# Stores of an attention-score kernel, given in turn to the SyncE and the ScalarE DMA queue

## Chip, cores and metric

One NeuronCore of a Trainium2 chip runs the kernel. The metric is the device time of one execution in microseconds (us), as the median of several runs; executions of one kernel here mostly agree within 0.3%. A ratio in this text is the mean time of one kernel's fast runs over the mean time of the fast runs of the kernel before, taken in the same rounds on the same chip, so it is not quite the ratio of the medians quoted beside it. "Stretch" means a window of the profiled span, and a "packet" is one piece of a transfer as the profile lists it (16 KB of a store, 8 KB of a load).

## The reference

```python
batch, heads, seq, dim = 8, 8, 512, 64
def reference(q, k):                      # q, k: float32 [8, 8, 512, 64]
    scale = 1.0 / np.sqrt(q.shape[-1])
    return np.einsum('bhqd,bhkd->bhqk', q, k) * scale   # float32 [8, 8, 512, 512]
```

16.8 MB come in, 67.1 MB go out.

## The kernel before

Two batches at a time are a group (4 groups, `v`). Of each group, q and k are loaded (4 loads of 1 MB), cast to bf16 and transposed through TensorE. Then 8 output tiles (`c`) of 2 MB each are computed: TensorE into PSUM (the memory that holds its results), evicted (copied out, and scaled) half by ScalarE and half by VectorE into a tile `o`, and stored with one transfer. There are 5 buffers of `o`. In the text the 32 output tiles are numbered from 0 in program order.

```python
    raw_pool = ctx.enter_context(tc.tile_pool(name="raw", bufs=4))
    out_pool = ctx.enter_context(tc.tile_pool(name="out", bufs=5))
    psum_pool = ctx.enter_context(tc.tile_pool(name="psum", bufs=3, space=bass.MemoryType.PSUM))
    # ... (cut)
    def evacuate(dst, src):               # in turn ScalarE, VectorE
        nonlocal n_evac
        if n_evac % 2 == 0:
            nc.scalar.mul(out=dst, in_=src, mul=scale)
        else:
            nc.vector.tensor_scalar(out=dst, in0=src, scalar1=scale, scalar2=None,
                                    op0=mybir.AluOpType.mult)
        n_evac += 1
    # ... (cut: load_and_cast issues all 16 loads with nc.sync; transpose)
    def scores(v, c, kT, qz):
        o = out_pool.tile([P, RO, S], f32, name="o")
        for i in range(0, RO, 2):
            ps = psum_pool.tile([P, 2, S], f32, name="ps")
            for w in range(2):
                nc.tensor.matmul(out=ps[:, w, :], lhsT=qz[:, i + w, c, :],
                                 rhs=kT[:, c].rearrange("d m j -> d (m j)"),
                                 start=True, stop=True)
            evacuate(o[:, i:i + 2, :], ps)
        nc.sync.dma_start(out=out_r[v, c], in_=o.rearrange("p i k -> p (i k)"))
    # ... (cut: loads of all groups first; transposes of group v + 1 after tile 3 of group v)
```

Of the kernel before, what the change touches and what calls it, by code (L numbers as in the profile page):

```python
# [1 line left out]

# [5 lines left out]


@with_exitstack  # L10
def kernel(
    ctx: ExitStack,
    tc: tile.TileContext,
    q: bass.AP,
    k: bass.AP,
    out: bass.AP,
):






    nc = tc.nc
    B, H, S, D = q.shape
    scale = 1.0 / (D ** 0.5)
    P = 128
    UNITS = B // 2
    N = H // 2
    C = 2 * N  # L30
    M = P // H
    R = S // M
    RO = 8
    U = S // RO
    JJ = R // RO
    IW = 8 // JJ

    f32 = mybir.dt.float32
    bf16 = mybir.dt.bfloat16

    q_r = q.rearrange("(v x) g (m j) d -> v x (g m) (j d)", x=2, j=R)
    k_r = k.rearrange("(v x) g (m j) d -> v x (g m) (j d)", x=2, j=R)
    out_r = out.rearrange("(v x) (n h) (u i) k -> v (x n) (h u) (i k)", x=2, h=2, i=RO)

    consts = ctx.enter_context(tc.tile_pool(name="consts", bufs=1))
    raw_pool = ctx.enter_context(tc.tile_pool(name="raw", bufs=4))
    bf_pool = ctx.enter_context(tc.tile_pool(name="bf", bufs=5))
    t_pool = ctx.enter_context(tc.tile_pool(name="t", bufs=2))
    out_pool = ctx.enter_context(tc.tile_pool(name="out", bufs=5))
    tpsum_pool = ctx.enter_context(tc.tile_pool(name="tpsum", bufs=2, space=bass.MemoryType.PSUM))  # L50
    psum_pool = ctx.enter_context(tc.tile_pool(name="psum", bufs=3, space=bass.MemoryType.PSUM))

    n_evac = 0

    def evacuate(dst, src):
# [8 lines that stand above are left out]
    def load_and_cast(v):  # L64

        both = []
        for src in (k_r, q_r):
            xb = bf_pool.tile([P, R, 2, D], bf16, name="xb")
            for x in range(2):
                xf = raw_pool.tile([P, R * D], f32, name="xf")  # L70
                nc.sync.dma_start(out=xf, in_=src[v, x])  # L71
                if v > 0:
                    copy = nc.gpsimd.tensor_copy
                else:
                    copy = (nc.vector.tensor_copy, nc.scalar.copy)[x]
                copy(out=xb[:, :, x, :], in_=xf.rearrange("p (j d) -> p j d", j=R))  # L76
            both.append(xb)
        return both

    def half(h):  # L80
        return slice(h * D, (h + 1) * D)

    def clear(engine, qz, h):

        engine.memset(qz[half(h), :, :, (1 - h) * U:(2 - h) * U], 0.0)  # L85

    def transpose(v, kb, qb):

        kT = t_pool.tile([P, C, M, R], bf16, name="kT")
        qz = qzs[v % 2]  # L90
        for j0 in range(0, R, 8):
            tp = tpsum_pool.tile([P, 8, P], bf16, name="tp")
            for j in range(8):
                nc.tensor.transpose(out=tp[:, j, :], identity=identity,  # L94
                                    in_=kb[:, j0 + j].rearrange("p x d -> p (x d)"))
            for x in range(2):
                for h in range(2):
                    copy = (nc.vector.tensor_copy, nc.scalar.copy)[h]
                    copy(out=kT[half(h), x * N:(x + 1) * N, :, j0:j0 + 8],  # L99
                         in_=tp[half(x)].rearrange("d j (n h m) -> d h n m j", n=N, h=2)[:, h])  # L100
        for i0 in range(0, RO, IW):
            tp = tpsum_pool.tile([P, IW, JJ, P], bf16, name="tp")
            for i in range(IW):
                for jj in range(JJ):
                    nc.tensor.transpose(out=tp[:, i, jj, :], identity=identity,  # L105
                                        in_=qb[:, RO * jj + i0 + i].rearrange("p x d -> p (x d)"))
            for x in range(2):
                for h in range(2):
                    copy = (nc.vector.tensor_copy, nc.scalar.copy)[h]
                    copy(out=qz[half(h), i0:i0 + IW, x * N:(x + 1) * N, h * U:(h + 1) * U]  # L110
                         .rearrange("d i n (m jj) -> d i n m jj", jj=JJ),
                         in_=tp[half(x)].rearrange("d i jj (n h m) -> d h i n m jj", n=N, h=2)[:, h])
        return kT, qz
# [8 lines that stand above are left out]
                                 rhs=kT[:, c].rearrange("d m j -> d (m j)"),  # L122
                                 start=True, stop=True)
            evacuate(o[:, i:i + 2, :], ps)
        nc.sync.dma_start(out=out_r[v, c], in_=o.rearrange("p i k -> p (i k)"))

    cast = [load_and_cast(0)]
    identity = consts.tile([P, P], dtype=bf16)
    make_identity(nc, identity)
    qzs = [consts.tile([P, RO, C, P], bf16, name=f"qz{n}") for n in range(2)]  # L130
    clear(nc.vector, qzs[0], 0)
    clear(nc.gpsimd, qzs[0], 1)
    for x in range(2):
        clear(nc.gpsimd, qzs[1], x)
    for v in range(1, UNITS):
        cast.append(load_and_cast(v))

    ts = {0: transpose(0, *cast[0])}
    for v in range(UNITS):
        for c in range(C):  # L140
            scores(v, c, *ts[v])
            if c == C // 2 - 1 and v + 1 < UNITS:
                ts[v + 1] = transpose(v + 1, *cast[v + 1])


# [1 line left out]
_INS = ['q', 'k']  # L147
_OUTS = [((8, 8, 512, 512), 'float32')]


# [23 lines left out]
```

## Time and profile before

| | before |
|---|---|
| time, median of 3 | 204.38 us (204.25 to 204.42) |
| profiled span | 203.2 us |
| DMA queue q1, share of 16 engines | 97.3% |
| VectorE, ScalarE, PE busy | 63%, 52%, 52% |
| store, issue to landing | 20.5 us (median) |

No compute engine is busy for more than two thirds of the span, and the one DMA queue for nearly all of it.

### The profile page before, as it was taken

What the parts mean: (1) busy time and instruction counts of PE and PEld (TensorE: products, weight loads), DVE (VectorE), ACT (ScalarE), POOL (GpSimd) and SP (SyncE); (2) the same over time, 40 slices, a digit from 0 to 9 for tenths busy, and PEclk for the clock granted to TensorE, in tenths of its full rate; (3) what the DMA queues carried; (4) which work ended last, traced back from release to release, by engine and by line L of the source; (5) the groups of instructions that cost most, each with busy time, mean ns of one, the idle gap of its engine ahead of it and who ended that gap; (6) DMA issues with size and microseconds to landing.
All of it is one profiled execution on the core that took longest, in us unless ns stands there. A gap on an engine that the chain in (4) does not pass through costs nothing.

```text
span 203.2 us, 1530 instructions
## 1 busy us (share of the span) xinstructions
PE 105.0 (52%) x512; PEld 48.5 (24%) x512; DVE 128.3 (63%) x131; ACT 104.8 (52%) x131; POOL 34.8 (17%) x21
## 2 busy tenths in 40 slices
PE   0033579873388535979555938545455755610000
PEld 0033334332352213533122413112121211200000
DVE  3793778997769989779678889444444444440000
ACT  2317668866676867688384787333333333330000
POOL 8957777706000000000000000000000000000000
PEclk9999999999559999699988699997975597575555
DMA  6999999999999999999999999999999999999990
GB/s 226 427 411 429 421 426 423 419 424 426 432 435 426 435 423 423 439 429 426 435 432 423 435 426 432 435 423 439 429 424 435 426 429 435 429 429 439 423 419 35
DMA packets 6919, 83.98 MB, mean 413 GB/s; under 512 B 768, under 2 KB 768, under 8 KB 768
## 3 DMA queue, kind: packets, MB, share of 16 engines
q1 hardware_dynamic: 6912, 83.89, 97.3%
q8 instruction: 4, 0.07, 0.1%
q14 instruction: 3, 0.02, 0.0%
HBM read 16.78 MB, written 67.11 MB: 413 GB/s over the span
## 4 chain that ended last, share of the span: by engine, by line
DMA 42%; DVE 17%; PE 15%; ACT 13%; issue 1%; SPq 0%; ACTq 0%
DMA out_dram<-o 38%; PE ps L121 9%; DVE o L60 8%; ACT o L58 6%; DMA xf<-in_q_dram 4%; DVE kT L99 4%; ACT kT L99 4%; PE tp L105 4%; DVE qz L110 3%; PE tp L94 3%; ACT qz L110 2%; DVE xb L76 2%; ACT xb L76 1%; SPq L71 0%; ACTq L58 0%
## 5 line engine op out<-in xcount | busy, mean ns | idle before, releaser
L121 PE MATMUL ps<-kT,qz 128*128 128x512 bf16 x256 | 82.3, 450 | 38.2 <-ACT o L58 30.6
L60 DVE TENSOR_SCALAR o<-ps 128x1024 f32<-128x1024 f32 x64 | 77.5, 1223 | 36.2 <-DMA out_dram<-o 22.1
L58 ACT ACTIVATE o<-ps 128x1024 f32<-128x1024 f32 x64 | 63.2, 1022 | 40.7 <-DMA out_dram<-o 34.7
L121 PEld LDWEIGHTS <-qz 128*128 128x128 bf16 x256 | 27.3, 109 | 86.7 <-issue 70.4
L99 ACT COPY kT<-tp 64x512 bf16<-64x512 bf16 x32 | 18.4, 579 | 15.6 <-DVE kT L99 11.6
L110 DVE COPY qz<-tp 64x512 bf16<-64x512 bf16 x32 | 21.5, 686 | 6.5 <-PE tp L105 6.2
L76 POOL CAST xb<-xf 128x2048 bf16<-128x2048 f32 x12 | 22.7, 1893 | 15.5 <-PE tp L94 7.0
L94 PE MATMUL tp<-identity,xb 128*128 128x128 bf16 x128 | 12.5, 261 | 24.0 <-ACT kT L99 11.1
L110 ACT COPY qz<-tp 64x512 bf16<-64x512 bf16 x32 | 18.2, 579 | 12.1 <-DVE qz L110 11.4
L99 DVE COPY kT<-tp 64x512 bf16<-64x512 bf16 x32 | 21.3, 684 | 5.0 <-PE tp L94 4.4
L105 PE MATMUL tp<-identity,xb 128*128 128x128 bf16 x128 | 12.4, 263 | 12.6 <-ACT kT L99 7.3
L94 PEld LDWEIGHTS <-xb 128*128 128x128 bf16 x128 | 10.9, 121 | 27.5 <-issue 16.3
L105 PEld LDWEIGHTS <-xb 128*128 128x128 bf16 x128 | 11.0, 121 | 16.6 <-issue 15.4
L85 POOL MEMSET qz<- 64x4096 bf16 x3 | 11.5, 3830 | 0.1
L76 DVE CAST xb<-xf 128x2048 bf16<-128x2048 f32 x2 | 7.2, 3604 | 3.7 <-DMA xf<-in_k_dram 2.6
L76 ACT CAST xb<-xf 128x2048 bf16<-128x2048 f32 x2 | 3.8, 1897 | 6.1 <-DMA xf<-in_k_dram 6.0
L85 DVE MEMSET qz<- 64x2048 uint32 x1 | 1.8, 1765 | 1.2 <-PEq L158 1.2
L76 ACT ACT_TABLE_LOAD x1 | 1.3, 1283 | 0.7 <-PEq L158 0.7
masks.py:199 POOL TENSOR_SCALAR_AFFINE_SELECT identity<-identity 128x128 bf16<-128x128 bf16 x1 | 0.3, 292 | 0.1
masks.py:197 POOL MEMSET identity<- 128x128 bf16 x1 | 0.2, 204 | 0.3 <-POOLq L158 0.3
L158 POOL MEMSET const-float32-0.0<- 128x1 f32 x1 | 0.1, 103 | 0.2 <-issue 0.2
L158 POOL MEMSET const-bfloat16-1.0<- 128x1 bf16 x1 | 0.1, 111 | 0.0
(2 smaller groups left out, 0.2 us busy)
## 6 DMA issues: line engine op xcount, KB each, us to landing
out_dram<-o SPq DMA_DIRECT2D x32, 2048.0 KB, 20.5
xf<-in_k_dram SPq DMA_DIRECT2D x8, 1024.0 KB, 7.9
xf<-in_q_dram SPq DMA_DIRECT2D x8, 1024.0 KB, 8.4
```

The lines of the kernel that those rows point to most:

```text
L58: nc.scalar.mul(out=dst, in_=src, mul=scale)
L60: nc.vector.tensor_scalar(out=dst, in0=src, scalar1=scale, scalar2=None, op0=mybir.AluOpType.mult)
L76: copy(out=xb[:, :, x, :], in_=xf.rearrange("p (j d) -> p j d", j=R))
L85: engine.memset(qz[half(h), :, :, (1 - h) * U:(2 - h) * U], 0.0)
L94: nc.tensor.transpose(out=tp[:, j, :], identity=identity, in_=kb[:, j0 + j].rearrange("p x d -> p (x d)"))
L99: copy(out=kT[half(h), x * N:(x + 1) * N, :, j0:j0 + 8], in_=tp[half(x)].rearrange("d j (n h m) -> d h n m j", n=N, h=2)[:, h])
L105: nc.tensor.transpose(out=tp[:, i, jj, :], identity=identity, in_=qb[:, RO * jj + i0 + i].rearrange("p x d -> p (x d)"))
L110: copy(out=qz[half(h), i0:i0 + IW, x * N:(x + 1) * N, h * U:(h + 1) * U] .rearrange("d i n (m jj) -> d i n m jj", jj=JJ), in_=tp[half(x)]. ...
L121: nc.tensor.matmul(out=ps[:, w, :], lhsT=qz[:, i + w, c, :], rhs=kT[:, c].rearrange("d m j -> d (m j)"), start=True, stop=True)
L158: nc = _bacc.Bacc("TRN2", target_bir_lowering=False, num_devices=1)
```

## The change

The intent is to spread the stores over two issuing engines, so that neither the issuing nor one queue's order holds them back.

```diff
-        nc.sync.dma_start(out=out_r[v, c], in_=o.rearrange("p i k -> p (i k)"))
+        queue = (nc.sync, nc.scalar)[c % 2]
+        queue.dma_start(out=out_r[v, c], in_=o.rearrange("p i k -> p (i k)"))
```

## The prediction

> **What bounds the kernel now.** I read the page from the fullest resource down: the 40 slices, the DMA queues and issues, the chain that ended last, SyncE's own waits, then a table of stretches for the end. First the slices, queues and issues:
>
> ```profile
> DMA  6999999999999999999999999999999999999990
> GB/s 226 427 411 429 421 426 423 419 424 426 432 435 426 435 423 423 439 429 426 435 432 423 435 426 432 435 423 439 429 424 435 426 429 435 429 429 439 423 419 35
> ...
> q1 hardware_dynamic: 6912, 83.89, 97.3%
> q8 instruction: 4, 0.07, 0.1%
> ...
> out_dram<-o SPq DMA_DIRECT2D x32, 2048.0 KB, 20.5
> ```
>
> The DMA engines stand at nine tenths or more in all slices but the first and the last, and no slice moves more than 439 GB/s. All 16 loads and 32 stores are on one queue, q1, whose packets fill 97.3% of 16 engines' span. A store takes 20.5 us from issue to landing, though 2 MB at 430 GB/s is 4.9 us: some four stores stand in line.
>
> Next, the waits of SyncE (us in total, times, longest):
>
> ```profile
> SPq L125 <- DVE o L60: 132.9, 31, 15.0
> SPq L169 <- DMA out_dram<-o: 20.7, 5, 4.8
> ```
>
> And some steps of the chain that ended last, in order of time (start, length):
>
> ```profile
> 85.33 0.02 SPq L125
> ...
> 85.38 12.88 DMA out_dram<-o
> 98.28 0.04 ACTq L58
> 98.32 0.04 issue
> 98.36 1.03 ACT o L58
> ```
>
> SyncE never waits to issue a store for anything but VectorE's last eviction of that tile: 132.9 us of idle waiting. What it spends on issuing is 32 times some 0.33 us. The chain from 85 us on is a store, an eviction that wanted its buffer, the next store: compute waits for the DMA engines, not they for compute. (Before 85 us the chain runs through compute, but the slices show the DMA engines full there too.)
>
> Last, the stretches at the end (stretch, PE, PEld, DVE, ACT and POOL busy, granted clock, DMA share, GB/s):
>
> ```profile
> 181.00:200.00 19.00, 0.00 (x0) 0.00 (x0) 0.05 (x1) 0.00 (x0) 0.00 (x0) 0.50 0.91 392
> 200.00:201.00 1.00, 0.00 (x0) 0.00 (x0) 0.00 (x0) 0.00 (x0) 0.00 (x0) 0.50 0.08 33
> 201.00:202.00 1.00, 0.00 (x0) 0.00 (x0) 0.00 (x0) 0.00 (x0) 0.00 (x0) 0.50 0.04 16
> ```
>
> Compute ends at 181 us; the last 21 us are the queue emptying. From 200 to 202 us about one engine of 16 (0.06) still works: one engine is behind the others. The trace has 4 packets of 16 KB of instruction fetch, at 38, 70, 106 and 155 us, of 0.88 to 1.11 us each; they sum to 3.8 us, which about fits the 3 us by which one engine outlasts the rest, if all four fell on it.
>
> **What the Trainium skill says.** "DMA: Bandwidth & Descriptors", section "Issuing engines are not separate DMA queues": transfers started from SyncE, ScalarE or GpSimd run on the same 16 engines and interleave; issuing from several saves only the sequencer's time to start them. This trace agrees with the second half as far as one queue can: 0.33 us of issue against 4.9 us of data. Same page, "Queues, rings and completion order": an engine takes turns between the queues that have work, a packet at a time. No run here shows it yet; I use it for the order of landings. Same page, "Where 436 GB/s comes from": 435 GB/s is the ceiling of the 16 ports. The trace agrees: 423 to 439 GB/s, or a median 611 ns for a 16 KB packet, times 16 engines 429 GB/s. "Perfetto Trace Analysis", section "DMA Optimizations", advises spreading over issuing engines when "the bottleneck is descriptor generation"; SyncE's waits above say that it isn't.
>
> **The change, part by part.** Bytes do not change. Per DMA engine a store is 8 packets of 611 ns and a load 8 packets of 309 ns (medians of the trace), so 32 x 8 x 0.611 = 156.4 us and 16 x 8 x 0.309 = 39.6 us, with 48 semaphore packets of 9 ns 0.4: 196.4 us. The first packet starts at 1.75 us, so an undelayed engine ends at 198.2 us; the last one ends at 201.9, its store has landed at 202.4, the span ends at 203.2, and the measured time is 1.2 us more. Of these terms the change touches none: 196.4 of data, 1.75 at the start, 3.7 of the late engine, 2.5 from its last packet to the measured end: 204.4.
>
> What it removes: 16 issues from SyncE, 16 x 0.33 = 5.3 us, all in SyncE's 133 us of idle. Worth 0. It adds them to ScalarE, which is busy 104.8 of 203 us: 5.3 us, 3% of its span. In the stretch from 85 us on ScalarE waits for DMA anyway. Worth 0.
>
> What it moves: ScalarE now executes in order a store that waits for VectorE. In the built order the store of an odd tile stands behind the first eviction of the next tile, some 1 us later, so VectorE's last eviction (1.22 us) is mostly done; but that first eviction itself waits for a buffer. With 5 buffers, three other tiles are then still in the queues, 3 x 4.9 = 14.7 us, so the delay is not seen by the DMA engines. The built schedule also mixes the transposes of the next head group with evictions, where before they stood in a block.
>
> The tightest place is the first turn of the buffers. At 36.6 us, when tile 1's store goes out on ScalarE, about 7.5 us of loads (landing at 44.1) are ahead of tile 0's store on SyncE's queue. Taking turns, tile 1 and then tile 3 pass it. Loads and five stores are 7.5 + 5 x 4.9 = 32 us of work, which ends at 68.4 us in the kernel before (the fifth store's landing), and must here. Tile 0 can land as late as 68.4 - 2 x 4.9 = 58.6, with tiles 2 and 4 behind it (in the built program tile 2's store also waits for tile 1's to have landed); before, it landed at 49.0. Tile 5 wants tile 0's buffer, and its first eviction stands in ScalarE's order before most of the second group's transposes. From 58.6 its path to the store is, on ScalarE, four evictions of 1.02 us (tiles 5 and 6 alternate) and five copies of 0.58: 7.0 us, with some 0.5 us for waits on VectorE and PE, so it issues at about 66.1. An issue's first packet came 1.0 us after it at the start of the kernel (issue 0.75, packet 1.75), so data at 67.1: 1.3 us before the queues are empty. A narrow escape by this estimate; if I have missed 2 or 3 us of waits, a gap of 1 to 2 us opens once. Afterwards a group of 8 tiles needs about 31 us of VectorE (16 x 1.22 + 16 x 0.69) against 39 us of DMA, so the lead grows again. I put 0.3 us into the sum for this, and -0.2 for bubbles between stores that two queues may hide (a store landed every 4.94 us on average against 8 x 0.611 = 4.89, mostly the late engine's). Sum: 204.4 + 0.3 - 0.2 = 204.5 us.
>
> **Rivals.** First, two queues overlap better and it gets faster. [...]Against: [...]the packets cover 97.3% of the span, and the rate is at the port's ceiling. Even with all bubbles and half of the late engine gone it would be some 202 us. Second, blocking in ScalarE's order starves the engines, in the first turn as above or at each group: a gap of 1 to 3 us, one to three times, 206 to 210 us. For: transposes and evictions share ScalarE, and the lead had fallen to 8 us at 60 and 85 us (12.9 us to landing less the store's own 4.9). Against: the lead never fell below that, and work in the queues is conserved whichever is served first. Third, alternating queues makes each packet dearer, or loads and stores mixed disturb each other. 3% on stores would be 156.4 x 0.03 = 4.7 us, so 209. Nothing in this trace speaks for it: the 9 ns semaphore packets already stand between 16 KB ones without a visible gap.
>
> **Range and chances.** The kernel repeats within 0.1%, so the width is mine: low end 203.2 for hidden bubbles, high end 206.8 for one gap of 2 us. Faster by over 2% means under 200.3, which is below 196.4 + 1.75 + 2.5 = 200.7 even with the late engine cured: 1%. Slower by over 2% is above 208.5 and needs a repeated gap or dearer packets: 7%. The rest, 92%, is within 2%.
>
> **What would show it.** Right: two queues with 16-engine shares that sum to 97%, all slices at 9, GB/s as before, store landing still near 20 us, compute ending near 181 us, one late engine at the end. Tile 0's store landing after tile 1's, near 58 us, would confirm the turn-taking. Wrong: a slice under 9 between 60 and 75 us or at a later transposition (second rival); 16 KB packets over 620 ns where both queues are full (third); ScalarE's wait for DMA growing matters only if a slice dips with it.

## More of the kernel before

A scheduler orders each engine's instructions when the kernel is built, and a pool decides then which buffer a tile gets. So a change of one line can move instructions elsewhere.

## The result

| | before | changed |
|---|---|---|
| time, median of 4 | 204.40 us (204.25 to 204.78) | 204.37 us (203.98 to 204.45) |
| ratio, 95% interval | | 0.9992 (0.9973 to 1.0011) |
| profiled span | 203.2 us | 202.4 us |
| DMA queues, share of 16 engines | 97.3% | 59.0% + 38.8% = 97.8% |
| ScalarE busy | 104.8 us | 106.1 us |

The time is the same. The slices, queues and issues of the changed kernel's page:

```profile
DMA  5999999999999999999999999999999999999992
GB/s 215 429 413 424 429 423 418 385 428 436 431 440 424 424 444 418 428 437 428 424 437 431 424 434 431 428 437 431 424 431 437 428 424 437 424 431 440 424 428 120
...
q1 hardware_dynamic: 4608, 50.33, 59.0%
q10 hardware_dynamic: 2304, 33.56, 38.8%
...
out_dram<-o SPq DMA_DIRECT2D x16, 2048.0 KB, 18.4
out_dram<-o ACTq DMA_DIRECT2D x16, 2048.0 KB, 16.2
```

Two queues now carry what one carried, all slices but the ends stay at nine, and the rate is where it was. The eighth slice (385 GB/s, 35 to 40 us) is not idle: loads and stores run together there for the first time, and some 8 KB packets took longer: the 99th percentile of all of them is 574 ns, against 471 before, while the median stays at 309.

Did the queues take turns? One microsecond in which both had work, in the changed kernel's DMA view (queue, packets, MB, share):

```profile
q10 hardware_dynamic: 19, 0.31, 72.6%
q1 hardware_dynamic: 19, 0.16, 36.7%
```

From 42 to 43 us, 19 packets of loads and 19 of stores: packet for packet, so the stores with their 16 KB packets get two thirds of the bytes. This agrees with the Trainium skill, "DMA: Bandwidth & Descriptors", section "Queues, rings and completion order". The consequence: tile 1's store, issued beside the loads, landed at 48.4 us, tile 3's at 58.1, and tile 0's, behind the loads on the other queue, only at 59.1 (before: 53.9, 63.6 and 49.0).

And what did ScalarE's in-order issuing do? Its timeline in the changed kernel (start, length, what, idle before and what ended it):

```profile
51.06 1.02 ACT L58 ACTIVATE o<-ps 128x1024 f32<-128x1024 f32 x1
52.10 0.58 ACT L99 COPY kT<-tp 64x512 bf16<-64x512 bf16 x1
58.22 1.02 ACT L58 ACTIVATE o<-ps 128x1024 f32<-128x1024 f32 x1 [5.53 <-DMA out_dram<-o]
...
60.40 0.34 ACTq L126 DMA_DIRECT2D out_dram<-o  x1
```

The first line is ScalarE's last eviction for tile 5. VectorE ended its own for that tile at 54.5 us. The store of tile 5 could have gone out then, but in ScalarE's order two evictions for tile 6 stand first, and the first of them waited until 58.2 for a buffer. The store left at 60.4: 5.9 us late. Yet in the stretches around it the DMA engines never lacked work (stretch, PE, PEld, DVE, ACT, POOL busy, granted clock, DMA share, GB/s):

```profile
36.00:60.00 24.00, 12.48 (x66) 5.65 (x66) 16.11 (x18) 13.83 (x18) 7.41 (x4) 0.84 1.02 423
60.00:75.00 15.00, 9.97 (x43) 4.86 (x42) 11.15 (x12) 7.11 (x10) 0.00 (x0) 0.68 1.00 429
...
85.00:181.00 96.00, 58.65 (x272) 25.36 (x272) 68.02 (x70) 58.45 (x71) 0.00 (x0) 0.88 1.01 430
```

So the change did have a cost, and the line of stores before the DMA engines hid it. Such a delay was rare: of ScalarE's 16 stores this one left 5.9 us after its tile was ready, one left 1.2 us after, and the others within 0.4 us. What also shrank is the lead, by which I mean the work that is issued to the DMA engines and not yet moved when a store is issued. Counted from the packets, at 429 GB/s, its lowest was 6.0 us in the kernel before (at 85.4 us) and 3.9 us in the changed one (at 97.6 us).

### The profile page after: what moved, and what is told of

The parts are those of the page before. It is cut to its first block, busy times and chain, and to the rows that moved or that the text cites. A ratio compares the mean times of both kernels' runs of the same rounds, so it can differ in the third digit from the quotient of the medians.

```text
span 202.4 us, 1499 instructions
## 1 busy us (share of the span) xinstructions
PE 103.4 (51%) x512; PEld 48.2 (24%) x512; DVE 127.9 (63%) x131; ACT 106.1 (52%) x131; POOL 34.9 (17%) x21
## 3 DMA queue, kind: packets, MB, share of 16 engines
q10 hardware_dynamic: 2304, 33.56, 38.8%
## 4 chain that ended last, share of the span: by engine, by line
DMA 30%; DVE 23%; PE 19%; ACT 14%; issue 4%; SPq 0%; DVEq 0%; ACTq 0%
DMA out_dram<-o 26%; DVE o L60 17%; PE ps L121 14%; ACT o L58 8%; DMA xf<-in_q_dram 4%; PE tp L105 3%; ACT qz L110 3%; ACT kT L99 3%; DVE qz L110 2%; DVE kT L99 2%; PE tp L94 2%; DVE xb L76 2%; ACT xb L76 1%; SPq L71 0%; DVEq L60 0%
## 5 line engine op out<-in xcount | busy, mean ns | idle before, releaser
L121 PE MATMUL ps<-kT,qz 128*128 128x512 bf16 x256 | 84.9, 447 | 59.1 <-DVE o L60 42.6
L58 ACT ACTIVATE o<-ps 128x1024 f32<-128x1024 f32 x64 | 64.5, 1023 | 38.4 <-DMA out_dram<-o 21.8
L121 PEld LDWEIGHTS <-qz 128*128 128x128 bf16 x256 | 26.7, 109 | 103.4 <-issue 89.1
L99 ACT COPY kT<-tp 64x512 bf16<-64x512 bf16 x32 | 18.4, 579 | 13.2 <-DVE kT L99 10.7
L94 PE MATMUL tp<-identity,xb 128*128 128x128 bf16 x128 | 12.3, 253 | 17.5 <-ACT xb L76 10.1
L94 PEld LDWEIGHTS <-xb 128*128 128x128 bf16 x128 | 10.5, 115 | 22.1 <-ACT xb L76 10.1
L105 PE MATMUL tp<-identity,xb 128*128 128x128 bf16 x128 | 13.4, 271 | 3.0 <-ACT kT L99 2.1
L105 PEld LDWEIGHTS <-xb 128*128 128x128 bf16 x128 | 12.0, 126 | 8.4 <-issue 6.9
## 6 DMA issues: line engine op xcount, KB each, us to landing
out_dram<-o SPq DMA_DIRECT2D x16, 2048.0 KB, 18.4
out_dram<-o ACTq DMA_DIRECT2D x16, 2048.0 KB, 16.2
```

The lines of the kernel that those rows point to most:

```text
L94: nc.tensor.transpose(out=tp[:, j, :], identity=identity, in_=kb[:, j0 + j].rearrange("p x d -> p (x d)"))
L99: copy(out=kT[half(h), x * N:(x + 1) * N, :, j0:j0 + 8], in_=tp[half(x)].rearrange("d j (n h m) -> d h n m j", n=N, h=2)[:, h])
L105: nc.tensor.transpose(out=tp[:, i, jj, :], identity=identity, in_=qb[:, RO * jj + i0 + i].rearrange("p x d -> p (x d)"))
L121: nc.tensor.matmul(out=ps[:, w, :], lhsT=qz[:, i + w, c, :], rhs=kT[:, c].rearrange("d m j -> d (m j)"), start=True, stop=True)
```

## Experiments

My theory: the DMA engines' data set the time, so who issues is indifferent as long as compute stays ahead; the in-order issuing and the turn-taking eat into that lead, which 5 buffers provide. Rivals: a gain of two queues is there but cancelled by a loss; or alternation is free in itself.

### All stores on ScalarE

```diff
-        nc.sync.dma_start(out=out_r[v, c], ...)
+        nc.scalar.dma_start(out=out_r[v, c], ...)
```

> Edit: all 32 stores on ScalarE's queue, loads stay on SyncE's. Theory (the DMA engines bound the kernel, and who issues does not matter): 204.4 us, within 0.5%, all slices at 9 tenths, loads stretched while stores run beside them. Rival A (the gain of a second queue is there, but eaten by ScalarE's in-order blocking): with all 32 store issues on ScalarE the blocking doubles against 16, so 1% or more slower than before. Rival B (a second queue hides bubbles between transfers): loads beside stores for the first 50 us, so up to 1 us faster.

Measured: 205.53 us (203.91 to 206.73, 4 runs), ratio 1.0045 (0.9990 to 1.0099). By the time alone this is between the theory and rival A, and not a decision; rival B is not supported. The profile says more:

```profile
out_dram<-o ACTq DMA_DIRECT2D x32, 2048.0 KB, 10.9
```

From issue to landing a store takes 10.9 us: two stores stand in line, where SyncE alone kept four and alternation between three and four. In the stretch from 140 to 160 us the DMA share fell to 0.91 for the first time in a kernel with 5 buffers. The lead is down to 0.2 us there (at 156.2 us): it starts to run out. Late stores are not what used it up, since all 32 left within 0.4 us of their tile being ready; compute as a whole ran less far ahead, and why is not shown.

### A quarter of each store: the DMA bound taken away

Three quarters of the output are not written.

```diff
-        nc.sync.dma_start(out=out_r[v, c], in_=o.rearrange("p i k -> p (i k)"))
+        nc.sync.dma_start(out=out_r[v, c, :, :2 * S],
+                          in_=o[:, :2, :].rearrange("p i k -> p (i k)"))
```

> Wrong result on purpose: each store writes only the first quarter of its tile (512 KB), all on SyncE. Takes the DMA bound away: data per engine falls from 196 to about 196.4 - 0.75 x 156.4 = 79 us, so compute sets the time. Theory: 140 to 160 us (VectorE's 128 us plus the start of some 15 us), no waits of evictions for stores; this is the base for the alternating kernel beside it.

Measured: 152.57 us (151.10 to 153.25), as expected. The same cut in the changed kernel:

> Wrong result on purpose: the same quarter stores, going alternately to SyncE's and ScalarE's queues. Shows what the change costs where the DMA engines do not hide it. Theory: ScalarE gets 16 issues of 0.33 us, 5.3 us, and is not the busiest engine, so 0 to 5 us over the quarter kernel with SyncE alone. Rival A (in-order blocking of ScalarE is a real cost, hidden in the full kernel by the DMA bound): over 5 us slower. If it is faster, the reshuffled schedule is worth more than the issues cost.

Measured: 149.01 us (148.92 to 149.02), ratio to the kernel before 0.7285 against 0.7451, so 2.2% faster than SyncE alone. The expectation was missed on the good side: where compute is the bound, the issues cost nothing visible. VectorE's busy time is nearly the same (126.5 and 125.9 us), so 2.9 of the 3.5 us of span are idle time of VectorE that went away, most of it between 50 and 75 us (21.4 and 23.9 us busy there). The build ordered the instructions differently, and TensorE's granted clock in that stretch was 0.80 with SyncE alone and 1.00 with alternation. Which of the two it was I did not separate. What the pair does show is that 16 store issues on ScalarE (338 ns each in the full changed kernel, median) weigh less than these two together.

### Three and two output buffers: the lead taken away

```diff
-    out_pool = ctx.enter_context(tc.tile_pool(name="out", bufs=5))
+    out_pool = ctx.enter_context(tc.tile_pool(name="out", bufs=3))     # and 2
```

> Kernel before with 3 output buffers in place of 5. The lead of compute over the DMA engines was 8 us at its lowest with 5 buffers; two buffers fewer take 9.8 us of it, so about 2 us of starvation at each of the transposition stretches: 206 to 212 us.

> Changed kernel (alternating queues) with 3 output buffers. Theory (the change is neutral only because the lead of 5 buffers hides ScalarE's in-order issuing and the later landings of taking turns): slower than SyncE alone with 3 buffers, by 1 to 5%. Rival (alternation is neutral by itself, buffers or no): within 1% of SyncE alone with 3 buffers. Second rival (the second queue keeps the engines fed better): faster than it.

> Kernel before with 2 output buffers. One tile is filled while one is stored: per tile 4.9 us of data and some 4 us of compute overlap, but every transposition stretch (9 to 11 us of copies per group of 8) starves the DMA engines: 220 to 240 us, slices below 9.

> Changed kernel (alternating queues) with 2 output buffers. Theory (ScalarE issues an odd tile's store behind the first eviction of the next tile, and that eviction waits for the previous store to land): the two stores hardly overlap, so 3% or more slower than SyncE alone with 2 buffers. Rival (neutral by itself): within 1% of it.

| buffers | SyncE alone | ratio | alternating | ratio | alternating over SyncE alone |
|---|---|---|---|---|---|
| 5 | 204.40 us | 1 | 204.37 us | 0.999 | 0.999 |
| 3 | 208.41 us | 1.0207 | 216.46 us | 1.0603 | 1.039 |
| 2 | 220.71 us | 1.0803 | 226.71 us | 1.1093 | 1.027 |

The last column is the quotient of the two ratios. Without the lead, alternation loses 3.9% and 2.7%. (At 2 buffers I had expected 3% or more; the sign is as expected, the size a little under, and the mechanism is not the expected one: no store on ScalarE left more than 0.1 us after its tile was ready. The two kernels with SyncE alone lie within their ranges.) The rivals "neutral by itself" and "the second queue feeds them better" fall for these buffer counts. Where the time goes with 3 buffers, in slices of 5.2 us (SyncE alone) and 5.4 us (alternating):

```profile
DMA  6999999999979999987999999889999999999994
```

```profile
DMA  6999999999950999999999999999798999899996
```

SyncE alone has shallow dips at each of the three transposition stretches. Alternation has one deep hole. Its stretches:

```profile
60.00:65.00 5.00, 0.00 (x0) 0.00 (x0) 0.68 (x1) 0.72 (x1) 0.00 (x0) 0.50 0.38 161
65.00:70.00 5.00, 4.40 (x22) 2.58 (x23) 4.03 (x6) 3.64 (x6) 0.00 (x0) 0.50 0.00 0
```

From 65 to 70 us no byte moves. Adding up, between the first packet and the last, the time for which the 16 engines' packets do not account (611 ns a store packet, 309 a load packet) gives 8.6 us for SyncE alone and 15.8 us for alternation, of which 8.7 us lie between 60 and 80 us. Late issuing on ScalarE did not make this hole: its two stores before it left within 0.1 us of their tiles being ready.

### What of alternation costs, with 3 buffers

Three kernels take it apart. First, no alternation, all stores on ScalarE (`nc.scalar` as above, with `bufs=3`):

> 3 output buffers, one queue for all stores, but ScalarE issues all 32. No two stores take turns; every store stands in ScalarE's order. If the 3.9% that alternation lost with 3 buffers (216.5 against 208.4 us) comes from ScalarE's in-order issuing, this has twice as many such issues and is at least as slow as alternation: 216 to 224 us. If it comes from two stores taking turns, this is near SyncE alone: 208 to 211 us.

Measured: 215.69 us (214.19 to 217.87), ratio 1.0528 of the fast runs (one of four was slow). About as alternation, if a little under it, where I had said at least as slow. Second, alternation with GpSimd in place of ScalarE:

```diff
-        queue = (nc.sync, nc.scalar)[c % 2]
+        queue = (nc.sync, nc.gpsimd)[c % 2]
```

> 3 output buffers, stores alternate between SyncE's and GpSimd's queues; GpSimd has no evictions, so an eviction never stands behind a store, but two stores still take turns. If in-order issuing on ScalarE is the cause: 207 to 211 us, near SyncE alone (208.4). If taking turns is the cause: 214 to 218 us, near alternation with ScalarE (216.5). Confounded a little: GpSimd's casts can stand behind a store in the first 60 us, which could cost a few us there.

Measured: 217.50 us (214.56 to 218.93), ratio 1.0564 (1.0483 to 1.0646; one of four was slow). Also about as alternation, though no eviction can stand behind a store here; but 3.2 us of the loss lie between 20 and 40 us, where a cast stood behind the first store on GpSimd and the loads that wanted its buffer left up to 9 us later, so the run is confounded as feared. Third, SyncE alone, with ScalarE only waiting for VectorE where it would have issued:

```diff
+    probe = consts.tile([P, 1], f32, name="probe")
     ...
+        if c % 2 == 1:
+            nc.scalar.copy(out=probe, in_=o[:, RO - 1, S - 1:S])
         nc.sync.dma_start(out=out_r[v, c], in_=o.rearrange("p i k -> p (i k)"))
```

> 3 output buffers, all stores on SyncE's one queue; for odd tiles ScalarE makes a copy of one column of the tile's last eviction by VectorE, at the place where the changed kernel has it issue the store: ScalarE's wait for VectorE without the store. If the mere wait for VectorE is the cause: 212 to 217 us. If what costs is the store itself being issued late (behind a blocked eviction) or taking turns, this is near SyncE alone: 208 to 210 us.

Measured: 208.19 us (207.69 to 208.69), ratio 1.0186. The wait for VectorE costs nothing. So neither turn-taking between stores nor ScalarE is needed for a loss, and the wait is not it: my either-or was too narrow. What the three losing kernels share is that stores leave the loads' queue. Their gaps do not lie alike. With all stores on ScalarE there are several dips in place of one hole:

```profile
DMA  6999999999999889999976899998799899999994
```

There the built kernel uses the three buffers in turn, as SyncE alone does; no run explains that loss. In the built alternating kernel with 3 buffers (and in the one with GpSimd), tile 4 gets the buffer of tile 3, whose store landed at 64.2 us, although tile 0's buffer was free from 54.5 us. A last run removes that choice:

```diff
-    out_pool = ctx.enter_context(tc.tile_pool(name="out", bufs=3))
+    out_pools = [ctx.enter_context(tc.tile_pool(name=f"out{n}", bufs=1)) for n in range(3)]
     ...
-        o = out_pool.tile([P, RO, S], f32, name="o")
+        o = out_pools[(v * C + c) % 3].tile([P, RO, S], f32, name="o")
```

> Alternating queues with 3 output buffers, but the buffers are three pools of one, used strictly in turn (tile n takes that of tile n-3). In the alternating kernel with 3 buffers from one pool, the build gave tile 4 the buffer of tile 3, whose store landed at 64.2 us, while that of tile 0 lay free from 54.5 us on; the DMA engines stood still from 64 to 70 us. If this choice of buffers (and the order of instructions that comes with it) is the cause of the larger part of the loss: no hole there and 208 to 212 us. If alternation itself is the cause: 215 to 218 us again, with the hole.

Measured: 211.61 us (209.81 to 212.28, 6 runs), ratio 1.0366 (1.0348 to 1.0384). The hole is gone:

```profile
60.00:65.00 5.00, 3.02 (x12) 1.15 (x12) 3.10 (x4) 2.84 (x3) 0.00 (x0) 1.00 0.99 419
65.00:70.00 5.00, 1.93 (x7) 0.57 (x6) 3.06 (x3) 2.15 (x3) 0.00 (x0) 1.00 0.99 419
```

Of the 8.1 us that alternation lost (216.5 less 208.4), the choice of buffers and the order that came with it account for 4.9. Buffers in turn also put the second group's transposes back into a block. And in the kernel with the hole, tile 2's store waited 10.3 us for tile 1's to land, because the build had given both the same completion semaphore; here it did not wait. The three are not separated. The other 3.2 us stay with alternation. The profiled run was one of the two short ones (209.81 us), so it does not show all of them; its deepest dip is at 140 to 160 us, a DMA share of 0.85 against 1.00 for SyncE alone. Late issuing did not make that dip: from 100 to 175 us every store left within 0.7 us of its tile being ready (elsewhere two on ScalarE left 4.4 and 4.7 us late). The stores of tiles 17 and 18, before the dip, stood on the two queues together and landed 12.9 and 12.7 us after issue (9.0 and 6.4 with SyncE alone), and tile 20 had to wait for tile 17's buffer. That fits turn-taking, but no run isolates it.

### More PE instructions: the late DMA engine

```diff
             for w in range(2):
+                for _ in range(2):
+                    nc.tensor.matmul(out=ps[:, w, :16], lhsT=qz[:, i + w, c, :],
+                                     rhs=kT[:, c].rearrange("d m j -> d (m j)")[:, :16],
+                                     start=True, stop=True)
                 nc.tensor.matmul(out=ps[:, w, :], ...)
```

> Kernel before, plus two matmuls of 16 columns ahead of each score matmul, whose results the real one overwrites: 512 more matmuls and 512 more weight loads, 1024 PE instructions, as many again as the kernel has, so 4 more 16 KB instruction fetches. Tests the late DMA engine. Theory (the end is set by the one DMA engine that also fetches PE's instructions, 0.95 us each): 4 x 0.95 = 3.8 us longer, 208.2 us. Rival (the late engine is late for another reason, or fetches go to another engine): 204.4 us. If the additional PE work itself starved the DMA engines, a slice would fall below 9.

Measured: 206.54 us (206.34 to 206.56), ratio 1.0096 (1.0079 to 1.0113). The page shows the fetches, 4 more than before, and the stretches at the end show again about one engine of 16 at work after the others:

```profile
q8 instruction: 8, 0.13, 0.2%
```

```profile
201.00:202.00 1.00, 0.00 (x0) 0.00 (x0) 0.00 (x0) 0.00 (x0) 0.00 (x0) 0.50 0.08 33
202.00:203.00 1.00, 0.00 (x0) 0.00 (x0) 0.00 (x0) 0.00 (x0) 0.00 (x0) 0.50 0.08 33
```

Longer, as the theory says, and no slice before the end fell below 9; but by 2.0 us (0.0096 x 204.4), not 3.8: half a microsecond a fetch in place of 0.95. I had taken a fetch's duration (0.88 to 1.11 us) for its cost. The engine moves a store's packet in the same time, as turns are taken, so I estimate that 16 KB cost at most one packet's 0.61 us. In the kernel before, the late engine's last four packets ended alone, 2.4 us after the rest, as 4 fetches of 0.61 would have it; here it was five packets, 3.0 us, for 8 fetches, and the rest ended a microsecond later too. But the changed kernel also made 4 fetches, and its last engine ended only two packets (1.2 us) after the rest. The trace does not name the engine of a packet, so whether all fetches fall on one engine is open, and the added matmuls were not tested without the fetches: that the fetches are the cause is not shown.

## Why the prediction was right

Its main step, that the sum of packet times, start and late engine is not touched, held: 97.3% of engine time before, 97.8% after, 16 KB packets at a median of 611 ns in both and on both queues. So did its refusal of the first rival: two queues found no gap to fill. The third (dearer packets) falls by the same 611 ns. One engine was again the last, by two packets (1.2 us) in place of four, which is the 0.8 us by which the span got shorter, about; it lies within what the runs of one kernel differ by. Two readings were off. The middle slices of the kernel before lie between 411 and 439 GB/s, not 423 and 439. And the span of 203.2 us belongs to a profiled execution that took 204.96 us, not the median 204.4: the measured time was 1.8 us more than its span, not 1.2. That the sum met the median to 0.1 us has half a microsecond of luck in it.

That issuing is worth nothing either way held: 338 ns an issue on ScalarE, 16 of them, in an engine busy for 52%; the quarter-store pair agrees.

Taking turns was right, even in the number: tile 0's store landed at 59.1 us, where I had "near 58 us", after tile 1's. Tile 2's store waited for tile 1's landing, as read from the build. The sign "store landing still near 20 us" did not come: it was 18.4 and 16.2 us.

The step on the tightest place was right in kind and wrong in its parts. I had tile 5 wait for tile 0's buffer until 58.6 us and its store leave at 66.1. In fact the build gave tile 5 the buffer of tile 1, free at 48.4 us, and tile 6 that of tile 3; tile 5 was ready at 54.5 and its store left at 60.4, held up by tile 6's evictions. The real lead at that point was larger than my 1.3 us, and the 0.3 us I had put into the sum for a gap did not appear. I had read the build's semaphores for tile numbers.

The second rival, a lead that runs out, was the one with substance. The blocking is real but rare (5.9 us for one store), and with 3 buffers alternation costs 3.9%. The part of my argument that ruled it out at 5 buffers, a lead of 8 us at its lowest, measured the wrong thing. I had read it from issue to landing (12.9 us at the shortest before, 12.4 after). But a store has landed when its last engine is done (for the one issued at 85.4 us, 2.3 us after its first), and with two queues that time also holds work that was issued later on the other queue. By the packets the lead was 6.0 us at its lowest before and 3.9 us after. Nor did it "grow again" after the first turn of the buffers: it was 6.8 us when tile 5's store left at 60.4 us, but 3.9 at 97.6 and 4.1 at 107.1 us, so "three other tiles are then still in the queues" did not hold there. The rival failed with 3.9 us to spare, which the prediction had not worked out: that part was luck.

The compute's end was not where I had it: the last store was issued at 184.3 us, not near 181. The lead at that store was 9.9 us, against 12.7 at the last store before, which nobody had to pay for.

## What to carry to other kernels

When one queue keeps all DMA engines at their rate, a second queue has nothing to add; look at the share of the queue and at the lead before spreading issues, and with two queues count the lead in bytes, as issue-to-landing time overstates it. Moving stores to an engine that also computes can make a store wait behind that engine's blocked work (here one of 16 by 5.9 us) and changes what the build does elsewhere. It costs nothing while enough work stands in line, so test such a change with fewer buffers to see what it really does. And after any move of stores, look up which buffer each tile gets and which store waits for another's landing: in the 3-buffer kernel, buffers in turn, with the order that came along, won back 4.9 of 8.1 us.

## What the Trainium skill lacked or had wrong

- "DMA: Bandwidth & Descriptors", "Issuing engines are not separate DMA queues": right that two queues add no bandwidth (ratio 0.9992), but it does not say what an issue can cost on an engine that also computes. Here one store of 16 left 5.9 us after its tile was ready.
- The same page, "Queues, rings and completion order": turns by packet agree (19 and 19 packets in 1 us). It draws no consequence for sizes: 16 KB store packets got twice the bytes of 8 KB load packets, and the last load landed at 51.3 us in place of 44.1.
- "Runtime: NRT & Kernel Launch", "Instruction fetch mechanics": its 16 KiB blocks of 256 instructions agree (1024 more instructions, 4 more fetches), but it calls the cost of crossing a block's boundary "one DMA tail-bump, mostly hidden", and gives no time for it on the DMA engines. Here, where they are the bound, a kernel with 4 more fetches (and 512 more matmuls) took 2.0 us longer, and one DMA engine ended 2.4 us (before), 1.2 us (changed) and 3.0 us (more instructions) after the rest.
- "DMA: Bandwidth & Descriptors", "Where 436 GB/s comes from", says that for transfers between HBM and SBUF "the HBM side (~358) binds". With one core at work it did not: 413 GB/s over the whole span, 423 to 439 in most slices. The page's own note on single-core numbers agrees with the measurement.
